# Strassen's seven products for eight in half of the gate and up matrix products of a transformer block

## The chip, the cores and the metric

The kernel runs on one core of a Trainium2 chip. The metric is the time of one execution on the device, in microseconds (us). The core has a matrix engine (TensorE, PE in the profile, whose weight loads are the row PEld), a vector engine (VectorE, DVE), a scalar engine (ScalarE, ACT), GpSimd (POOL) and a queue engine that issues DMAs (SyncE, SP). Each runs its own instructions in the order in which they were built.

## The reference

Two transformer blocks run one after the other on 512 tokens of width 1024, in float32. The change touches only the second block, which has two layers with two SwiGLU networks each, so four in all:

```python
def swiglu(x, w_gate, w_up, w_down):
    return (jax.nn.silu(x @ w_gate) * (x @ w_up)) @ w_down
...
    for l in range(DEPTH_2):
        h = h + 0.5 * swiglu(rmsnorm_2(h, ffn1_norm[l]), ffn1_w_gate[l], ffn1_w_up[l], ffn1_w_down[l])
        ...
        h = h + 0.5 * swiglu(rmsnorm_2(h, ffn2_norm[l]), ffn2_w_gate[l], ffn2_w_up[l], ffn2_w_down[l])
```

Gate and up are matrices of 1024 x 2816, down is 2816 x 1024.

## The kernel before

Activations lie as eight tiles of 128 x 512 (128 of the 1024 features by all 512 tokens). Every matrix product is made from three matmuls (`acc`, L384): each operand is split into a high and a low part (`split`: ScalarE copies the high part, L327, and VectorE subtracts it, L328), and high x low, low x high and high x high are summed in PSUM.

`swiglu_hidden` goes over the hidden features in 11 pairs of 128-row tiles (index `mp`, 0 to 10). For a pair, `proj_a` makes the gate product: two weight units, each of four k tiles by 256 columns, are loaded by a DMA into a tile `raw` (three buffers), split into `wh` and `wl` (three buffers each), and used by 2 x 4 x 3 matmuls of 512 columns; so a product has 48 matmuls. Then the up product follows in the same way. When a gate tile is done, VectorE multiplies it by the norm (`g`, L1203) and ScalarE applies silu; when an up tile is done, VectorE makes two multiplications (`u`, L1209 and L1210) and the product is split into `uh` and `ul`. After the eleventh pair, `residual` multiplies all 22 hidden tiles with down, 256 output columns at a time, and VectorE adds the result to `h`.

The order on each engine is made by a scheduler from the order of the code and the free buffers. VectorE therefore works on splits for weights that TensorE needs one or two units later, in the gaps between the multiplications that wait for TensorE.

## Time and profile before

| | |
|---|---|
| median of three runs | 3082.12 us (3081.68 to 3083.63) |
| the profiled execution | 3079.62 us, of which the span from first to last instruction is 3077.8 us |
| TensorE busy | 3011.2 us, 98% of the span |
| VectorE busy | 1734.0 us, 56% |
| ScalarE busy | 1159.8 us, 38% |

The profiled execution is 2.50 us shorter than the median of the three runs, and 1.8 us of it lie outside the span. Busy time of TensorE counts overlapping matmuls once. A matmul's duration is longer than the distance to the next one, since matmuls are pipelined; what a matmul costs is read from the distance of two starts.

### The profile page before, as it was taken

The page shows a single profiled execution, that of the slowest core. Times are in us where ns is not written, and L with a number is a line of the kernel's source. Part 1 is how long each engine was busy: PE and PEld are TensorE (multiplying, and loading weights), DVE is VectorE, ACT ScalarE, POOL GpSimd, SP SyncE. Part 2 cuts the span into 40 slices and gives each one's busy share as a digit, 9 for nine tenths or more (in the row PEclk, how much of TensorE's full clock was granted, in tenths as well). Part 3 has the DMA queues.
Part 4 walks back from the last instruction along what each step waited for, and adds up shares of the span by engine and source line. Part 5 has one row for each costly group of instructions (what it writes and reads, how often), then busy time and mean ns, then how long its engine had stood idle before and what let it go on. Part 6 is the DMA issues. An engine that isn't in the chain of part 4 may idle for free.

```text
span 3077.8 us, 37929 instructions
## 1 busy us (share of the span) xinstructions
PE 3011.2 (98%) x14805; PEld 2501.5 (81%) x14805; DVE 1734.0 (56%) x2770; ACT 1159.8 (38%) x1794; POOL 171.1 (6%) x150
## 2 busy tenths in 40 slices
PE   9999999999999999999999999999999999999998
PEld 7778777888888888778888888888888788888888
DVE  5678666666454443587654433644435885644437
ACT  4454534444333322335333322433323353333225
POOL 0000221111000000112000000000000120000000
PEclk9999999999999999999999999999999999999999
DMA  6354324333233333333333333333333224333224
GB/s 206 119 130 131 100 82 129 93 102 96 93 93 110 96 95 97 97 91 86 109 100 96 96 96 99 100 103 96 93 96 106 84 69 126 93 98 98 91 95 152
DMA packets 309061, 318.69 MB, mean 104 GB/s; under 512 B 25230, under 2 KB 284005, under 8 KB 308882
## 3 DMA queue, kind: packets, MB, share of 16 engines
q1 hardware_dynamic: 303502, 307.24, 33.7%
q10 hardware_dynamic: 5380, 9.03, 1.0%
q8 instruction: 116, 1.90, 0.3%
q14 instruction: 63, 0.52, 0.1%
HBM read 289.77 MB, written 7.96 MB: 97 GB/s over the span
## 4 chain that ended last, share of the span: by engine, by line
PE 86%; DVE 7%; issue 3%; DMA 2%; ACT 2%; SPq 1%; POOL 1%; DVEq 0%; ACTq 0%; POOLq 0%
PE w L384 78%; DVE wl L328 2%; PE p L1419 1%; ACT wh L327 1%; PE p L762 1%; PE p L1512 1%; PE p L1580 1%; PE p L723 0%; PE p L769 0%; PE p L509 0%; DMA raw<-in_w_in_dram 0%; PE p L725 0%; PE p L1400 0%; DMA vec<-t5rows 0%; PE p L770 0%
## 5 line engine op out<-in xcount | busy, mean ns | idle before, releaser
L328 DVE TENSOR_TENSOR wl<-raw,wh 128x1024 fp32r<-128x1024 f32 (+3 forms) x524 | 634.6, 1211 | 874.2 <-ACT wh L327 863.1
L384 PE MATMUL w<-xl,wh 128*128 128x512 f32 (+1 forms) x2584 | 1000.9, 387 | 0.0
L384 PE MATMUL w<-xh,wh 128*128 128x512 f32 (+1 forms) x2584 | 998.5, 386 | 0.0
L384 PE MATMUL w<-xh,wl 128*128 128x512 f32 (+1 forms) x2584 | 998.1, 386 | 0.0
L327 ACT ACTIVATE wh<-raw 128x1024 fp32r<-128x1024 f32 (+3 forms) x524 | 537.8, 1026 | 1120.8 <-PE w L384 846.7
L384 PEld LDWEIGHTS w<-xl,wh 128*128 128x128 f32 x2584 | 487.0, 188 | 92.1 <-issue 0.6
L384 PEld LDWEIGHTS w<-xh,wh 128*128 128x128 f32 x2584 | 486.4, 188 | 92.1 <-issue 0.2
L384 PEld LDWEIGHTS w<-xh,wl 128*128 128x128 f32 x2584 | 486.7, 188 | 90.2
L384 PE MATMUL w<-uh,wl 128*128 128x512 f32 x880 | 342.3, 389 | 0.0
L384 PE MATMUL w<-ul,wh 128*128 128x512 f32 x880 | 342.3, 389 | 0.0
L384 PE MATMUL w<-uh,wh 128*128 128x512 f32 x880 | 342.3, 389 | 0.0
L384 PEld LDWEIGHTS w<-uh,wh 128*128 128x128 f32 x880 | 165.2, 188 | 34.4
L384 PEld LDWEIGHTS w<-ul,wh 128*128 128x128 f32 x880 | 165.2, 188 | 34.3
L384 PEld LDWEIGHTS w<-uh,wl 128*128 128x128 f32 x880 | 165.2, 188 | 34.2
L384 PE MATMUL w<-wh,xl 128*128 128x256 f32 (+2 forms) x480 | 141.2, 296 | 2.8 <-ACT wh L327 2.4
L384 PE MATMUL w<-wl,xh 128*128 128x256 f32 (+2 forms) x480 | 139.6, 291 | 0.0
L384 PE MATMUL w<-wh,xh 128*128 128x256 f32 (+2 forms) x480 | 137.8, 291 | 0.0
L1203 DVE TENSOR_TENSOR g<-w,R 128x512 f32<-128x512 f32 x88 | 60.5, 691 | 112.5 <-PE w L384 94.2
L327 ACT ACTIVATE uh<-u 128x512 fp32r<-128x512 f32 x88 | 55.7, 634 | 151.1 <-DVE u L1210 151.1
L303 ACT ACTIVATE g<-g 128x512 f32<-128x512 f32 (+1 forms) x112 | 65.8, 593 | 110.1 <-DVE g L1203 96.7
L384 PEld LDWEIGHTS w<-wh,xl 128*128 128x128 f32 x480 | 92.5, 193 | 7.3 <-ACT wh L327 2.6
L384 PEld LDWEIGHTS w<-wl,xh 128*128 128x128 f32 x480 | 92.8, 193 | 1.5 <-issue 0.7
(394 smaller groups left out, 3222.7 us busy)
## 6 DMA issues: line engine op xcount, KB each, us to landing
raw<-in_ffn_w_gate_dram SPq DMA_DIRECT2D x88, 512.0 KB, 3.8
raw<-in_ffn_w_up_dram SPq DMA_DIRECT2D x88, 512.0 KB, 3.8
raw<-in_ffn_w_down_dram SPq DMA_DIRECT2D x80, 512.0 KB, 3.5
raw<-in_w_in_dram SPq DMA_DIRECT2D x71, 512.0 KB, 3.9
raw<-in_w_up_dram SPq DMA_DIRECT2D x44, 512.0 KB, 3.5
raw<-in_w_gate_dram SPq DMA_DIRECT2D x32, 512.0 KB, 3.5
raw<-in_ple_w_gate_dram SPq DMA_DIRECT2D x24, 512.0 KB, 3.6
raw<-in_w_down_dram SPq DMA_DIRECT2D x20, 512.0 KB, 3.5
```

The source lines that it names most:

```text
L303: self.members.append(self.nc.scalar.activation(*args, **kw).ins)
L327: nc.scalar.activation(hi, src, AF.Copy)
L328: nc.vector.tensor_tensor(lo, src, hi.bitcast(F32), op=OP.subtract)
L384: mm(out, l, r, start=first and i == 0, stop=last and i == 2, skip_group_check=shared)
L762: nc.tensor.transpose(pt[:, i * P:(i + 1) * P], y[:, s * P:(s + 1) * P], self.ident)
L1203: nc.vector.tensor_tensor(t, p, x.R, op=OP.mult)
L1419: nc.tensor.matmul(p[:, t * 64:(t + 1) * 64].rearrange("p (n w) -> p n w", w=w), x[:, t * P:(t + 1) * P], v(x)[:, t * nb:(t + 1) * nb, 1], ...
L1512: nc.tensor.matmul(po[:, t * 64:(t + 1) * 64], sc[s][:, (t - s) * P:(t - s + 1) * P], V[s][:, hv], start=s == 0, stop=s == t)
L1580: nc.tensor.matmul(p[:, :n], q[h][:96, t * P:(t + 1) * P], k[h][:96, :n], start=True, stop=True)
```

## The change

In each of the four SwiGLUs the 11 pairs are cut into three parts (`THIRDS`: pairs 0 to 3, 4 to 7 and 8 to 10), and down is multiplied after each part, with the 8, 8 and 6 hidden tiles of that part; so `h` is added to three times.

Pairs 0, 1 and 2 stay as they were. From pair 3 on the gate product, and in pairs 4, 6, 8 and 10 the up product too, is made by `seven`: the product is seen as two by two blocks (two halves of k, two row tiles, two halves of the tokens), and seven block products of 4 x 3 matmuls with 256 columns take the place of eight. That is 84 matmuls of 256 columns for 48 of 512. For it the weights need four differences (`minus`) and seven splits of 128 x 512, and three additions in PSUM on VectorE and two copies of PSUM (`keep`) on ScalarE join the seven results. The activations need four sums and differences of their blocks, which `half_sums` makes once for each SwiGLU, after pair 1: 16 operations of 128 x 256 and 8 splits of 128 x 512, and first eight full-precision tiles, on ScalarE where the source is still there (`x.src`), and on VectorE in the first SwiGLU (L440), where it isn't.

`beside` interleaves the steps of the gate product with those of the up product of the same pair, so that other matmuls stand between a block product and the step that needs what VectorE or ScalarE makes of it.

```diff
--- before.py
+++ after.py
@@ -91,6 +91,11 @@
 KEEP = 2
 EARLY = 3
 LATE = 5.0, 8.0
+FF_SLOTS = dict(U=16, S=16, B=16, V4=4)
+THIRDS = (0, 1, 2, 3), (4, 5, 6, 7), (8, 9, 10)
+BESIDE = 0, 0, 1, 0, 1, 0, 0
+BOTH = 0, 0, 3, 0, 2, 0, 0
+PLAIN, UP = 3, (4, 6, 8, 10)
 MA, MB, YN = 13, 13, 8
 RAW, SPL = 3, 3
 AHEAD, EVAC, BEHIND = 1000, -1000, 1000
@@ -248,8 +253,9 @@
         return f"{s}{self.n}"
 
     PLACE = {"h": "H", "mix": "H", "xh": "X", "xl": "X", "mh": "X", "ml": "X", "uh": "U", "ul": "U",
+             "sxh": "S", "sxl": "S", "wb": "B", "wt4": "V4",
              "qk": "W", "V": "W", "rc": "W", "hq": "Q", "yh": "Y", "yl": "Y", "oh": "Y", "ol": "Y", "gate": "G"}
-    SHORT = ("R", "sq", "g", "u", "hd", "cv", "rows", "out", "lv", "rst", "rt")
+    SHORT = ("sv", "R", "sq", "g", "u", "hd", "cv", "rows", "out", "lv", "rst", "rt")
 
     def S(self, name="s", dt=F32):
 
@@ -418,6 +424,109 @@
                 yield nk * 3 * ncol * PASS
 
 
+    def half_sums(self, x, after):
+
+
+        nc, tt = self.nc, self.nc.vector.tensor_tensor
+        out = [([], []) for _ in range(4)]
+        for g in range(2):
+            f = {}
+            for k in (2 * g, 2 * g + 1, 2 * g + 4, 2 * g + 5):
+                f[k] = self.S("uh")
+                with self.after(after):
+                    if x.src:
+                        nc.scalar.activation(f[k], x.src[k], AF.Copy, scale=x.gain(k))
+                    else:
+                        tt(f[k], x.hi[k].bitcast(F32), x.lo[k].bitcast(F32), op=OP.add)
+            s = [self.S("uh") for _ in range(4)]
+            for i in range(2):
+                a, b = f[2 * g + i], f[2 * g + i + 4]
+                one, two, c = slice(0, 256), slice(256, 512), slice(256 * i, 256 * i + 256)
+                tt(s[0][:, c], a[:, two], b[:, two], op=OP.add)
+                tt(s[1][:, c], s[0][:, c], a[:, one], op=OP.subtract)
+                tt(s[2][:, c], a[:, one], a[:, two], op=OP.subtract)
+                tt(s[3][:, c], b[:, one], s[1][:, c], op=OP.subtract)
+            for t, (hi, lo) in zip(s, out):
+                h, l = self.S("sxh", F32R), self.S("sxl", F32R)
+                self.split(t, h, l)
+                for y, z in ((hi, h), (lo, l)):
+                    y += [z[:, :256], z[:, 256:]]
+        return out
+
+    def seven(self, W, c0, x, sums, evac):
+
+        nc, tt = self.nc, self.nc.vector.tensor_tensor
+        raw = []
+        for k0 in (0, 4):
+            t = self.rp.tile([P, 1024], F32, name=self.nm("raw"), tag="raw").rearrange("p (k c) -> p k c", k=4)
+            nc.sync.dma_start(t, W[k0 * P:(k0 + 4) * P, c0:c0 + 256].rearrange("(k p) c -> p k c", p=P))
+            raw += [t[:, :, :P], t[:, :, P:]]
+        b11, b12, b21, b22 = raw
+        both = [self.wp.tile([P, 1024], F32R, name=self.nm(n), tag=n) for n in ("wh", "wl")]
+        four = lambda t: t.rearrange("p (k c) -> p k c", k=4)
+
+        def minus(a, b):
+            t = four(self.S("wt4"))
+            tt(t, a, b, op=OP.subtract)
+            return t
+
+        def parts(src, at=None):
+            if at is None:
+                hi, lo = (four(self.S("wb", F32R)) for _ in range(2))
+            else:
+                hi, lo = (four(t[:, at * T:(at + 1) * T]) for t in both)
+            self.split(src, hi, lo)
+            return hi, lo
+        one, two = slice(0, 256), slice(256, 512)
+        cut = lambda k0, c: tuple([t[:, c] for t in y[k0:k0 + 4]] for y in (x.hi, x.lo))
+        bank, other = self.wps(), self.wps()
+        X, y, z, v = bank[:, one], bank[:, two], other[:, one], other[:, two]
+
+        def product(out, b, a, first=False):
+            for k in range(4):
+                self.acc(out, b[0][:, k], b[1][:, k], a[0][k], a[1][k], first and k == 0, k == 3, shared=True)
+            return 4 * 3 * 256 * PASS
+
+        def keep(p):
+            t = self.S("sv")
+            nc.scalar.activation(t[:, one], p, AF.Copy)
+            return t[:, one]
+        t1 = minus(b12, b11)
+        B11, T1 = parts(b11, 0), parts(t1)
+        t2 = minus(b22, t1)
+        T2, B21 = parts(t2), parts(b21, 1)
+        T3, B22 = parts(minus(b22, b12)), parts(b22)
+        T4 = parts(minus(b21, t2))
+        time = product(X, B11, cut(0, one), True)
+        p1 = keep(X)
+        yield time
+        time = product(z, T1, sums[0], True)
+        p5 = keep(z)
+        yield time
+        time = product(y, T2, sums[1])
+        tt(y, y, p1, op=OP.add)
+        tt(z, y, p5, op=OP.add)
+        yield time
+        yield product(X, B21, cut(4, one))
+        time = product(y, T3, sums[2])
+        tt(v, y, p5, op=OP.add)
+        yield time
+        time = product(z, B22, sums[3])
+        evac(1, other)
+        yield time
+        time = product(y, T4, cut(4, two))
+        evac(0, bank)
+        yield time
+
+    def beside(self, long, short, at):
+
+        for i, t in enumerate(long):
+            yield t
+            for _ in range(at[i]):
+                yield next(short)
+        yield from short
+
+
     def columns(self, parts, dma):
 
         nc = self.nc
@@ -456,9 +565,11 @@
             self.net, self.gain, self.scales = net, gain, scales
             self.hi, self.lo = [None] * KD, [None] * KD
             self.acc = [None] * len(scales)
+            self.src = [None] * KD
 
         def add(self, k, t):
             net, nc = self.net, self.net.nc
+            self.src[k] = t
             if self.gain is not None:
                 self.hi[k], self.lo[k] = net.S("xh", F32R), net.S("xl", F32R)
                 net.split(t, self.hi[k], self.lo[k], self.gain(k))
@@ -1183,40 +1294,57 @@
             norm.R, R1 = self.broadcast(norm.both)
             for k, t in enumerate(h):
                 nc.vector.scalar_tensor_tensor(t, t, self.col("norm_final_g", k), R1, op0=OP.mult, op1=OP.mult)
+        norm.src = None
         self.later((LATE[0], rows), (LATE[1], tile))
         return norm
 
 
     def swiglu(self, h, norm, which, l, nxt):
-        with self.phase({"W": 8}, U=44):
+        with self.phase({"W": 8}, **FF_SLOTS):
             self.swiglu_hidden(h, norm(), which, l, nxt)
 
     def swiglu_hidden(self, h, x, which, l, nxt):
         nc, a = self.nc, self.a
         Wg, Wu, Wd = (a[f"{which}_w_{n}_2"][l] for n in ("gate", "up", "down"))
-        uh, ul = [], []
-        for mp in range(11):
-            g = []
-
-            def evac_g(j, p, g=g):
-                t = self.S("g")
-                nc.vector.tensor_tensor(t, p, x.R, op=OP.mult)
-                self.act("silu", t, t, AF.Silu)
-                g.append(t)
-
-            def evac_u(j, p, g=g):
-                u = self.S("u")
+        uh, ul = [None] * KF, [None] * KF
+        first = []
+
+        def work(mp, sums):
+            g = [None] * 2
+
+            def evac_g(j, p):
+                g[j] = self.S("g")
+                first.append(nc.vector.tensor_tensor(g[j], p, x.R, op=OP.mult).ins)
+                self.act("silu", g[j], g[j], AF.Silu)
+
+            def evac_u(j, p):
+                u, m = self.S("u"), mp * 2 + j
                 nc.vector.tensor_tensor(u, p, x.R, op=OP.mult)
                 nc.vector.tensor_tensor(u, u, g[j], op=OP.mult)
-                hi, lo = self.S("uh", F32R), self.S("ul", F32R)
-                self.split(u, hi, lo)
-                uh.append(hi)
-                ul.append(lo)
-            self.push(self.proj_a(Wg, KD, [(mp * 256, 256)], x.hi, x.lo, evac_g))
-            self.push(self.proj_a(Wu, KD, [(mp * 256, 256)], x.hi, x.lo, evac_u))
+                uh[m], ul[m] = self.S("uh", F32R), self.S("ul", F32R)
+                self.split(u, uh[m], ul[m])
+            up = self.proj_a(Wu, KD, [(mp * 256, 256)], x.hi, x.lo, evac_u)
+            at = BESIDE
+            if sums and mp in UP:
+                up, at = self.seven(Wu, mp * 256, x, sums, evac_u), BOTH
+            if sums is None:
+                yield from self.proj_a(Wg, KD, [(mp * 256, 256)], x.hi, x.lo, evac_g)
+                yield from up
+            else:
+                yield from self.beside(self.seven(Wg, mp * 256, x, sums, evac_g), up, at)
+        sums = None
+        for third in THIRDS:
+            for mp in third:
+                self.push(work(mp, sums))
+                self.drain()
+                if mp == PLAIN - 2:
+                    made = self.half_sums(x, first[:1])
+                if mp == PLAIN - 1:
+                    sums = made
+            k = slice(third[0] * 2, third[-1] * 2 + 2)
+            self.push(self.residual(Wd[k.start * P:k.stop * P], k.stop - k.start, uh[k], ul[k], h, 0.5,
+                                    nxt=nxt if third is THIRDS[-1] else None))
             self.drain()
-        self.push(self.residual(Wd, KF, uh, ul, h, 0.5, nxt=nxt))
-        self.drain()
 
     def layer_consts(self):
         t = self.S("layer")
```

The order of all instructions outside the four SwiGLUs stays as it is, apart from line and buffer numbers. Two places inside show what moves.

The first is the third pair (`mp` 2) of the first SwiGLU. On VectorE before, the split `wl1691`, the second weight unit of this pair's up product, stands between the multiplications of the second pair (`u1671`) and the gate tiles of the third pair (`g1682`):

```order
L1209 TENSOR_TENSOR u1671_8015<-w1661_7947,R1632_7784 128x512
L1210 TENSOR_TENSOR u1671_8015<-u1671_8015,g1659_7943 128x512
L328 TENSOR_TENSOR wl1688_8095<-raw1686_8092,wh1687_8094 128x1024
L328 TENSOR_TENSOR ul1673_8019<-u1671_8015,uh1672_8018 128x512
L328 TENSOR_TENSOR wl1691_8125<-raw1689_8122,wh1690_8124 128x1024
L1203 TENSOR_TENSOR g1682_8072<-w1674_8022,R1632_7784 128x512
L1203 TENSOR_TENSOR g1683_8087<-w1675_8023,R1632_7784 128x512
```

After the change the same weight unit is called `wl1723`, and stands here (`sx` are the splits of the sums of activations, `wb` and `wl1733` split blocks of the fourth pair's gate weights, `wt4` is a difference of such blocks):

```order
L334 TENSOR_TENSOR sxl1699_8079<-uh1694_8066,sxh1698_8078 128x512
L1317 TENSOR_TENSOR g1714_8144<-w1706_8094,R1632_7784 128x512
L334 TENSOR_TENSOR sxl1701_8083<-uh1695_8067,sxh1700_8082 128x512
L1317 TENSOR_TENSOR g1715_8159<-w1707_8095,R1632_7784 128x512
L334 TENSOR_TENSOR sxl1703_8087<-uh1696_8068,sxh1702_8086 128x512
L334 TENSOR_TENSOR wl1723_8197<-raw1721_8194,wh1722_8196 128x1024
L334 TENSOR_TENSOR sxl1705_8091<-uh1697_8069,sxh1704_8090 128x512
L334 TENSOR_TENSOR wl1733_8243<-raw1730_8238,wh1732_8242 128x512
L334 TENSOR_TENSOR wb1738_8251<-wt41736_8246,wb1737_8250 128x512
```

The work of `half_sums` has come between: from the second pair's first `u` to this split VectorE now has 42 instructions (24 of 128 x 512, 16 of 128 x 256 and 2 of 128 x 1024), where it had 8.

On TensorE before, at the step from the first to the second weight unit of the third pair's up product:

```order
L384 MATMUL w1685_8091<-xh1550_7271,wl1688_8095 128x512
L384 MATMUL w1685_8091<-xh1550_7271,wh1687_8094 128x512
L384 MATMUL w1684_8090<-xl1575_7447,wh1690_8124 128x512
L384 MATMUL w1684_8090<-xh1574_7446,wl1691_8125 128x512
L384 MATMUL w1684_8090<-xh1574_7446,wh1690_8124 128x512
L384 MATMUL w1684_8090<-xl1579_7464,wh1690_8124 128x512
```

and after:

```order
L390 MATMUL w1717_8163<-xh1550_7271,wl1720_8167 128x512
L390 MATMUL w1717_8163<-xh1550_7271,wh1719_8166 128x512
L390 MATMUL w1716_8162<-xl1575_7447,wh1722_8196 128x512
L390 MATMUL w1717_8163<-xl1575_7447,wh1722_8196 128x512
L390 MATMUL w1734_8244<-xl1519_7065,wh1732_8242 128x256
L390 MATMUL w1735_8245<-sxl1683_8043,wb1737_8250 128x256
L390 MATMUL w1716_8162<-xh1574_7446,wl1723_8197 128x512
L390 MATMUL w1716_8162<-xh1574_7446,wh1722_8196 128x512
```

The matmuls with `wh1722` and, of the fourth pair's gate, with `wh1732` and `wb1737` are taken first, one of each, and then `w1716` needs `wl1723`.

The second place is the fourth pair of the second SwiGLU. On TensorE the third block product of the gate is followed by the first weight unit of the plain up product (`w2963`, `w2964`):

```order
L390 MATMUL w2945_14541<-sxh2911_14379,wb2952_14554 128x256
L390 MATMUL w2945_14541<-sxh2911_14379,wb2951_14553 128x256
L390 MATMUL w2963_14617<-xl2789_13824,wh2966_14621 128x512
L390 MATMUL w2964_14618<-xl2789_13824,wh2966_14621 128x512
L390 MATMUL w2963_14617<-xh2788_13823,wl2967_14622 128x512
L390 MATMUL w2963_14617<-xh2788_13823,wh2966_14621 128x512
```

and on VectorE its split `wl2967` stands behind the up tiles of the third pair:

```order
L334 TENSOR_TENSOR wb2955_14562<-wt42953_14559,wb2954_14561 128x512
L334 TENSOR_TENSOR ul2937_14513<-u2935_14509,uh2936_14512 128x512
L1323 TENSOR_TENSOR u2938_14528<-u2938_14528,g2926_14456 128x512
L334 TENSOR_TENSOR wb2957_14566<-raw2942_14537,wb2956_14565 128x512
L470 TENSOR_TENSOR wt42958_14569<-raw2942_14537,wt42950_14551 128x512
L334 TENSOR_TENSOR ul2940_14532<-u2938_14528,uh2939_14531 128x512
L334 TENSOR_TENSOR wl2967_14622<-raw2965_14619,wh2966_14621 128x1024
L334 TENSOR_TENSOR wb2960_14572<-wt42958_14569,wb2959_14571 128x512
L507 TENSOR_TENSOR w2945_14541<-w2945_14541,sv2961_14587 128x256
```

From the second pair's first `u` to `wl2967` VectorE has 51 instructions here (32 of 128 x 512, 16 of 128 x 256, 3 of 128 x 1024). The third and the fourth SwiGLU have the same order as the second at this place.

## Rows read from the trace of the kernel before

**Rows 1.** The page: busy time by engine, and the chain that ended last

```profile
PE 3011.2 (98%) x14805; PEld 2501.5 (81%) x14805; DVE 1734.0 (56%) x2770; ACT 1159.8 (38%) x1794; POOL 171.1 (6%) x150
...
PE 86%; DVE 7%; issue 3%; DMA 2%; ACT 2%; SPq 1%; POOL 1%; DVEq 0%; ACTq 0%; POOLq 0%
PE w L384 78%; DVE wl L328 2%; PE p L1419 1%; ACT wh L327 1%; PE p L762 1%; PE p L1512 1%; PE p L1580 1%; PE p L723 0%; PE p L769 0%; PE p L509 0%; DMA raw<-in_w_in_dram 0%; PE p L725 0%; PE p L1400 0%; DMA vec<-t5rows 0%; PE p L770 0%
```

**Rows 2.** Windows, second SwiGLU, gate and up, then down: stretch, length, busy, clock

```profile
1571.00:1799.00 228.00, 228.00 (x1008) 188.81 (x1007) 106.88 (x127) 70.32 (x85) 0.00 (x0) 1.00 0.33 98
1800.00:1921.00 121.00, 121.00 (x535) 100.19 (x535) 41.49 (x48) 32.54 (x40) 0.00 (x0) 1.00 0.29 91
```

**Rows 3.** Timeline of TensorE, second SwiGLU, first and 51st of 51 matmuls

```profile
1640.26 0.39 PE L384 MATMUL w<-xh,wh 128*128 128x512 f32 x1
...
1651.59 0.39 PE L384 MATMUL w<-xh,wl 128*128 128x512 f32 x1
```

**Rows 4.** Timeline of TensorE, last stage, first and 51st of 51 matmuls

```profile
3027.00 0.28 PE L384 MATMUL w<-xh,wh 128*128 128x256 f32 x1
...
3033.00 0.28 PE L384 MATMUL w<-xh,wl 128*128 128x256 f32 x1
```

**Rows 5.** Timeline of VectorE, first SwiGLU, the second pair's up tiles

```profile
936.09 0.69 DVE L1209 TENSOR_TENSOR u<-w,R 128x512 f32<-128x512 f32 x1 [0.35 <-PE w L384]
936.82 0.69 DVE L1210 TENSOR_TENSOR u<-u,g 128x512 f32<-128x512 f32 x1
938.21 0.69 DVE L328 TENSOR_TENSOR ul<-u,uh 128x512 fp32r<-128x512 f32 x1 [0.70 <-ACT uh L327]
938.82 0.68 DVE L1209 TENSOR_TENSOR u<-w,R 128x512 f32<-128x512 f32 x1
939.53 0.69 DVE L1210 TENSOR_TENSOR u<-u,g 128x512 f32<-128x512 f32 x1
940.14 1.22 DVE L328 TENSOR_TENSOR wl<-raw,wh 128x1024 fp32r<-128x1024 f32 x1
941.28 0.68 DVE L328 TENSOR_TENSOR ul<-u,uh 128x512 fp32r<-128x512 f32 x1
```

**Rows 6.** Groups by shape over the whole span: operation, count, busy us, mean ns

```profile
L327 ACT ACTIVATE uh<-u 128x512 fp32r<-128x512 f32 x88 | 55.7, 634 | 151.1 <-DVE u L1210 151.1
...
L1334 ACT ACTIVATE V<-w,y 128x256 f32<-128x256 f32 x32 | 14.9, 468 | 14.2 <-PE w L384 14.1
...
L1750 DVE TENSOR_TENSOR g<-w,R 128x256 f32<-128x256 f32 x16 | 6.3, 419 | 2.5 <-PE w L384 2.5
```

**Rows 7.** Timeline of TensorE around its wait at 480 us, first block

```profile
479.80 0.39 PE L384 MATMUL w<-mh,wh 128*128 128x512 f32 x1
484.00 0.79 PE L384 MATMUL w<-ml,wh 128*128 128x512 f32 x1 [3.81 <-DVE ml L1103]
484.59 0.63 PE L384 MATMUL w<-mh,wl 128*128 128x512 f32 x1
...
489.28 0.48 PE L384 MATMUL w<-ml,wh 128*128 128x512 f32 x1
489.60 0.40 PE L384 MATMUL w<-mh,wl 128*128 128x512 f32 x1
```

**Rows 8.** Windows of that wait: busy of PE, PEld, DVE, ACT, POOL, then PEclk

```profile
481.00:482.00 1.00, 0.00 (x0) 0.00 (x0) 1.00 (x3) 0.00 (x0) 0.00 (x0) 1.00 0.41 156
482.00:483.00 1.00, 0.00 (x0) 0.00 (x0) 1.00 (x2) 0.00 (x0) 0.87 (x1) 0.82 0.12 37
...
484.00:485.00 1.00, 1.00 (x2) 0.82 (x3) 1.00 (x1) 0.06 (x1) 1.00 (x1) 0.50 0.46 162
```

**Rows 9.** DMA issues by source: count, KB each, median us from issue to landing

```profile
raw<-in_ffn_w_gate_dram SPq DMA_DIRECT2D x88, 512.0 KB, 3.8
raw<-in_ffn_w_up_dram SPq DMA_DIRECT2D x88, 512.0 KB, 3.8
```

## Prediction

> **What bounds the kernel now.** I read the page first. TensorE is busy for 98% of the span, VectorE for 56%, and 86% of the chain that ended last lies on TensorE, 78% on the one line that issues the matmuls of the weight products [rows 1]. Then the stretch that is changed: over 228 us of gate and up and 121 us of down of the second SwiGLU TensorE is busy all the time at a granted clock of 1.00, while VectorE works 106.9 and 41.5 us and ScalarE 70.3 and 32.5 us [rows 2]. So a matmul that goes away here shortens the span by its distance to the next, as long as VectorE, ScalarE and the DMAs deliver in time; they have room on the whole, and the question is whether they have it at each place.
>
> **What a matmul costs.** Its bar (0.39 us) is not its cost. Fifty distances of matmuls with 512 columns take 11.33 us, 0.2266 us each [rows 3]. Fifty with 256 columns take 6.00 us, 0.1200 us each [rows 4]; this is the last stage, with weights stationary and half a tile of activations moving, as the change has it. Half the columns therefore cost 53%, not 50%. A plain product costs 48 x 0.2266 = 10.88 us, one by seven 84 x 0.1200 = 10.08 us: 0.80 us less, where counting multiplications promises an eighth, 1.36 us. In a SwiGLU 12 of 22 products change (8 gate, 4 up), in four SwiGLUs 48: **38.4 us** of TensorE time go away. Against this the Trainium skill (TensorE: Matmul & The Clock Gate, section "Back-to-back issue gap") gives the gap of an isolated warm matmul as columns over 2.4 GHz plus 2.5 ns; by it the products would cost 10.36 and 9.17 us, and the gain would be 57 us. The rows say otherwise: 0.2266 and 0.1200 us leave 13 ns beside the columns, and the sum goes by them.
>
> **What VectorE pays.** Neighbours that don't wait for each other start 0.61 us apart with 512 columns (938.21 to 938.82) and 1.14 us with 1024 (940.14 to 941.28), 0.08 us less than their bars; one that reads its neighbour's result starts 0.72 us after it [rows 5]. With 256 columns I take the bar of 0.42 us [rows 6] less the same 0.08, 0.34 us, between 0.31 (half of 0.61) and 0.42. A product by seven asks for 4 differences, 7 splits and 3 additions, 11 x 0.61 + 3 x 0.34 = 7.7 us, in the place of two weight splits of 1.14. A plain pair costs VectorE 4 x 1.14 + 2 x 0.61 for gate and 2 x (0.72 + 0.61 + 0.61) for up, 9.7 us of TensorE's 21.8. A pair with the gate by seven costs 15.1 us of 21.0, one with both 20.5 us of 20.2. A pair with both is thus just over what VectorE can do, but a gate-only pair or a down part (192 matmuls, 43.5 us, with 8 x 1.14 + 8 x 0.61 = 14 us of splits and additions) stands on either side. ScalarE has 14 splits at 0.63 us and 4 copies of PSUM at 0.47 [rows 6], with silu and hidden splits 13 us: no bound. The 16 further additions into `h` in a SwiGLU, and the weight blocks for the next pair, lie under the down matmuls.
>
> **Where TensorE will wait: the third and fourth pair.** Let T be the start of the second pair's up product. VectorE's first `u` there needs 36 matmuls and starts 0.19 us after them (the bar less the distance, 0.16, and a little; in [rows 5] it waits for just that): T + 8.35. What stands before it in VectorE's queue is done by then, so the queue can't start on `half_sums` earlier.
>
> In the first SwiGLU 42 instructions stand from there to the end of `wl1723`: 24 x 0.61 + 16 x 0.34 + 2 x 1.14 = 22.4 us, and 1.2 us for waits on ScalarE and a dependent neighbour, as in [rows 5] (0.70 and 0.12, and again in part). It is done at T + 31.9. TensorE has 122 matmuls of 512 columns and 2 of 256 before the one that needs it, 122 x 0.2266 + 2 x 0.12, and comes at T + 27.9: a wait of **4.0 us**. Behind `wl1723` wait the block splits of the fourth pair and the first weight unit of its up product, so the queue stays late and a second wait of some 1.5 us would follow. A wait of 3.8 us has its price in the first block: the clock was 1.00 in its second microsecond, 0.82 in the third and 0.50, the lower of its two levels (1.2 of 2.4 GHz), when the matmuls came back [rows 8], and 12 distances then took 5.28 us where 12 x 0.2266 = 2.72 was due [rows 7]: **2.6 us** lost. In that slow time VectorE catches up, so I count it in place of the second wait. First SwiGLU: 6.6 us.
>
> In the other three ScalarE makes the eight full-precision tiles, and 51 instructions stand up to `wl2967`: 32 x 0.61 + 16 x 0.34 + 3 x 1.14 = 28.4 us, and 1.9 us of waits (the same 1.2, and 0.7 until TensorE has the third pair's second up tile). Done at T + 38.6; TensorE comes at T + 144 x 0.2266 + 36 x 0.12 + 2 x 0.2266 = T + 37.4: **1.2 us**, three times, 3.6 us; so short a wait left the clock at 1.00 [rows 8].
>
> **The second and third parts.** Here I followed the order of VectorE, ScalarE and the raw tiles' DMAs row by row with the same prices. After a pair with both products the additions into PSUM that let the next pair's fourth block product start are done 0.1 us before TensorE asks, elsewhere 2 to 8 us before. VectorE loses some 4 us in each gate-only pair to the landing of a raw tile (3.8 us from issue, [rows 9]) which could be asked for only after its buffer's last split; that lies inside its lead. I charge 0.4 us for each of eight parts, 3.2 us, with bounds of 0 and 1.5 us. At the turn to down, the hidden tiles are due 7 us after the last up matmul and ready after some 4: nothing, and without that cover 4 us in each of 12 turns.
>
> **Sum.** 38.4 - 6.6 - 3.6 - 3.2 = 25.0 us. Against the profiled execution, 3077.8 + 1.8 = 3079.6, that is 3054.6; the median lies 2.5 us above that execution, so **3057 us**, 0.8% faster.
>
> **Rivals.**
> - *VectorE pays its whole bars* (0.69, 1.23 and 0.42 us, [rows 5, 6]) where operands are strided blocks or neighbours depend. Then the queues above take 25.7 + 1.2 and 32.5 + 1.9 us, the waits become 7.4 and 5.3 us, each with 2.6 us of clock and the first with 2 us more behind it: 12.0 + 3 x 7.9 = 35.7 us, and 1 us for each later part, 8: nothing of 38.4 is left, 3087 us, no change that can be told or slightly slower. Against it: 0.61 and 1.14 in [rows 5], on such splits. The Trainium skill (VectorE: DVE Perf Modes, section "The DRAIN you can't avoid") says that the next operation does not start until the pipe is empty, but that one which isn't held starts earlier; 938.21 to 938.82 shows the earlier start. 0.10.
> - *The raw buffers become the bound (slower).* Seven holds two of the three raw tiles until its last block is split, where a plain unit gave its one back after one split. If VectorE's lead is used up, each of the 32 products in the pairs with both shows its landing of 3.8 us [rows 9]. It decides at 25.0 / 32 = 0.8 us shown for each, beyond which the kernel is slower; with half the landing, 1.9 us, it is 61 - 25 = 36 us slower, 3118 us. For it: the three buffers, and only 0.1 us of lead after a pair with both. Against: the lead is 2 us and more at the other places, and DMA is busy a third of the time [rows 2]. 0.07.
> - *No wait anywhere.* VectorE finds its gaps, or ScalarE's tiles come sooner: 38.4 us, 3044 us. 0.12. The skill's gap, 57 us and thus 3025 us with no wait, has 0.01: [rows 3, 4] were read in this kernel.
> - *In between*: waits of 4 us and a slow clock in all four SwiGLUs, 25 to 33 us of 38.4, 3069 to 3077 us: 0.08.
>
> **How the numbers follow.** My forecast, with waits between 6 and 22 us (3050 to 3066 us), has 0.62. A measurement of this kernel tells some 0.2%, 6 us, from no change. Faster by more than that: 0.62 + 0.13 + 0.07 of the in-between = 0.82. Within: 0.01 of the in-between, 0.08 of the whole bars and 0.01 of the buffers, 0.10. Slower: 0.02 + 0.06 = 0.08. The range goes from no wait at all, 3043, to the worst in-between, 3077; it leaves out the skill's gap, the whole bars and the buffers, 0.18.
>
> **What the profile after would show.** TensorE's distances 0.120 us in the block products (right) or above 0.13 (wrong); the longest wait in the SwiGLUs, about 4 us, in the third pair of the first, released by VectorE's split L334, with PEclk at 0.50 behind it and nowhere else in a SwiGLU; waits of about 1 us in the fourth pair of the others; gate pairs 5 to 11 without a wait over 0.5 us. VectorE busy some 85 us longer for each SwiGLU (12 x 5.4 for the products, 10 for the sums, 10 for `h`). The prediction is wrong if the fourth pairs wait more than 4 us in every SwiGLU, if TensorE waits for a raw DMA, or if the block products' matmuls are spaced wider.

## The result, and the profile after

The changed kernel takes 3056.47 us (median of three runs, 3053.71 to 3058.94); its ratio to the kernel before is 0.9921, with a 95% interval of 0.9907 to 0.9934. That is 0.8% or 25 us faster. The prediction was 3057 us.

The page of the changed kernel's profile, its shortest execution (3053.71 us, of which the span is 3051.9); against [rows 1]:

```profile
PE 2976.9 (98%) x16533; PEld 2554.6 (84%) x16533; DVE 2073.3 (68%) x3514; ACT 1323.8 (43%) x2186; POOL 170.2 (6%) x150
...
PE 82%; DVE 9%; issue 4%; ACT 2%; DMA 2%; SPq 0%; POOL 0%; DVEq 0%; POOLq 0%; ACTq 0%
...
raw<-in_ffn_w_gate_dram SPq DMA_DIRECT2D x88, 512.0 KB, 4.3
raw<-in_ffn_w_up_dram SPq DMA_DIRECT2D x88, 512.0 KB, 3.9
```

TensorE is still busy for 98% of a span that is 25.9 us shorter. The raw tiles of gate and up land 4.3 and 3.9 us after their issue, in place of 3.8 [rows 9]. VectorE has 339 us more, 85 for each SwiGLU, as forecast. Its share of the chain that ended last has risen from 7 to 9%.

The second and third parts show the price of a block product. These are windows of the first SwiGLU of the changed kernel, pairs 4 to 7 and pairs 8 to 10 (columns as in [rows 2]):

```profile
1032.24:1114.60 82.36, 82.36 (x601) 78.47 (x600) 60.95 (x101) 37.84 (x63) 0.00 (x0) 1.00 0.32 98
1158.12:1219.45 61.33, 61.33 (x469) 59.38 (x468) 46.18 (x77) 29.54 (x49) 0.00 (x0) 1.00 0.30 93
```

Part two has 504 matmuls of 256 columns and 96 of 512: 504 x 0.1200 + 96 x 0.2266 = 82.2 us by [rows 3, 4], 82.36 measured, with TensorE busy from end to end and a clock of 1.00. Part three: 420 and 48, 61.3 worked out, 61.33 measured. By the gap of an isolated matmul that the Trainium skill gives (TensorE: Matmul & The Clock Gate, section "Back-to-back issue gap"), part two would by an estimate have taken 504 x 0.1092 + 96 x 0.2158 = 75.8 us; the trace does not agree with it here. The windows of parts two and three are as long in the other three SwiGLUs.

What TensorE waited for in the changed kernel, from the first SwiGLU to the fourth: the group of waits for weight splits (us in total, how many, the longest).

```profile
PE w L390 <- DVE wl L334: 8.1, 5, 3.6
```

The five waits of that group in the timeline of TensorE, each in the brackets of the matmul that waited:

```profile
955.74 0.28 PE L390 MATMUL w<-sxl,wb 128*128 128x256 f32 x1
959.61 0.50 PE L390 MATMUL w<-xh,wl 128*128 128x512 f32 x1 [3.58 <-DVE wl L334]
959.95 0.39 PE L390 MATMUL w<-xh,wh 128*128 128x512 f32 x1
...
963.82 0.40 PE L390 MATMUL w<-xh,wl 128*128 128x512 f32 x1
...
972.36 0.50 PE L390 MATMUL w<-xh,wl 128*128 128x512 f32 x1 [1.32 <-DVE wl L334]
...
1628.62 0.50 PE L390 MATMUL w<-xh,wl 128*128 128x512 f32 x1 [1.67 <-DVE wl L334]
...
2038.52 0.50 PE L390 MATMUL w<-xh,wl 128*128 128x512 f32 x1 [0.75 <-DVE wl L334]
...
2696.43 0.50 PE L390 MATMUL w<-xh,wl 128*128 128x512 f32 x1 [0.74 <-DVE wl L334]
```

The 3.58 us stand in the third pair of the first SwiGLU, before the matmul with `wl1723`, and 1.32 us more in its fourth pair; the others are in the fourth pairs of the other three. The timeline of VectorE before the first of them:

```profile
936.33 0.69 DVE L1322 TENSOR_TENSOR u<-w,R 128x512 f32<-128x512 f32 x1 [0.35 <-PE w L390]
...
946.16 0.42 DVE L447 TENSOR_TENSOR uh<-uh 128x256 f32<-128x256 f32 x1
946.49 0.42 DVE L448 TENSOR_TENSOR uh<-uh,uh 128x256 f32<-128x256 f32 x1
...
957.74 0.68 DVE L334 TENSOR_TENSOR sxl<-uh,sxh 128x512 fp32r<-128x512 f32 x1
958.34 1.22 DVE L334 TENSOR_TENSOR wl<-raw,wh 128x1024 fp32r<-128x1024 f32 x1
```

And the windows of a microsecond around its end, with the clock third from the right:

```profile
959.00:960.00 1.00, 0.39 (x2) 0.35 (x3) 1.00 (x2) 0.00 (x0) 0.00 (x0) 1.00 0.00 0
960.00:961.00 1.00, 1.00 (x5) 0.80 (x4) 1.00 (x3) 0.00 (x0) 0.00 (x0) 0.68 0.28 35
961.00:962.00 1.00, 1.00 (x4) 0.81 (x3) 1.00 (x3) 0.00 (x1) 0.00 (x0) 0.50 0.72 205
```

The prediction's T is the first row's start less 8.35, 927.98. VectorE ends `wl1723` at 959.56, T + 31.6 (forecast 31.9); TensorE asks at 956.02, T + 28.0 (forecast 27.9). The clock fell to 0.50 after TensorE had come back, and the eleven distances from 959.61 to 963.82 take 1.7 us more than 11 x 0.2266.

The idle time of the five waits and this 1.7 us make 9.8 us. What they cost is a little more: idle time is counted from the end of a bar, and bars are longer than distances. The starts of the matmuls give the whole loss. The table has the time from the first matmul of pair 0 to the end of pair 3 (to the next start behind its 384 or 420 matmuls), in the two timelines:

| SwiGLU | first | second | third | fourth |
|---|---|---|---|---|
| before, us | 89.99 | 88.12 | 88.74 | 88.12 |
| changed kernel, us | 96.37 | 89.44 | 89.05 | 88.39 |

One product by seven should have made each of these 0.8 us shorter; so 7.2, 2.1, 1.1 and 1.1 us are lost, 11.5 in all. Parts two and three lose 0.18 us in each SwiGLU, 0.7 in all, and 38.4 - 11.5 - 0.7 = 26.2 us are left.

Outside these products the two executions differ as well. The changed one takes 2.5 us less between them. Of this, 1.6 us lie before the second SwiGLU, where the clock fell for 3.4 us in the execution before (0.66 from 1294 to 1299 us) and did not in this one (1.00 from 1292 to 1297). It takes 0.2 us more ahead of the first SwiGLU and 2.6 us more in the last stage. There the first transposes wait 1.93 us for a small input, where they waited 0.94 us before, and the clock is lower behind it. The first of them in the timeline of TensorE:

```profile
2980.78 0.46 PE L683 MATMUL p<-ident,pin 128*128 128x128 f32 x2 [1.93 <-DMA pin<-in_p_dram]
```

### The profile page after: what moved, and what is told of

The parts are those of the page before. It is cut to its first block, busy times and chain, and to the rows that moved or that the text cites. A ratio compares the mean times of both kernels' runs of the same rounds, so it can differ in the third digit from the quotient of the medians.

```text
span 3051.9 us, 42727 instructions
## 1 busy us (share of the span) xinstructions
PE 2976.9 (98%) x16533; PEld 2554.6 (84%) x16533; DVE 2073.3 (68%) x3514; ACT 1323.8 (43%) x2186; POOL 170.2 (6%) x150
## 4 chain that ended last, share of the span: by engine, by line
PE 82%; DVE 9%; issue 4%; ACT 2%; DMA 2%; SPq 0%; POOL 0%; DVEq 0%; POOLq 0%; ACTq 0%
PE w L390 74%; DVE wl L334 2%; PE p L1547 1%; ACT wh L333 1%; PE p L873 1%; PE p L1640 1%; PE p L1708 1%; PE p L834 1%; PE p L880 0%; PE p L620 0%; PE p L836 0%; PE p L1528 0%; DMA dec<-in_decay_dram 0%; PE p L881 0%; PE p L1005 0%
## 5 line engine op out<-in xcount | busy, mean ns | idle before, releaser
L390 PE MATMUL w<-xh,wl 128*128 128x512 f32 (+1 forms) x2200 | 810.3, 368 | 8.1 <-DVE wl L334 8.1
L390 PE MATMUL w<-xl,wh 128*128 128x512 f32 (+1 forms) x2200 | 811.5, 369 | 0.0
L390 PE MATMUL w<-xh,wh 128*128 128x512 f32 (+1 forms) x2200 | 809.7, 368 | 0.0
L390 PEld LDWEIGHTS w<-xl,wh 128*128 128x128 f32 x2200 | 417.1, 190 | 62.3 <-issue 0.6
L390 PE MATMUL w<-sxh,wb 128*128 128x256 f32 x1536 | 282.0, 283 | 0.0
L390 PEld LDWEIGHTS w<-sxh,wb 128*128 128x128 f32 x1536 | 239.5, 192 | 0.6
L390 PE MATMUL w<-sxl,wb 128*128 128x256 f32 x768 | 217.4, 283 | 0.0
L333 ACT ACTIVATE wb<-wt 128x512 fp32r<-128x512 f32 x192 | 120.8, 630 | 121.4 <-DVE wt L470 87.2
L390 PEld LDWEIGHTS w<-sxl,wb 128*128 128x128 f32 x768 | 147.4, 192 | 0.7
L334 DVE TENSOR_TENSOR wb<-wt,wb 128x512 fp32r<-128x512 f32 x192 | 131.4, 684 | 13.2 <-ACT wb L333 13.2
```

The costliest lines, as they stand in the source:

```text
L333: nc.scalar.activation(hi, src, AF.Copy)
L334: nc.vector.tensor_tensor(lo, src, hi.bitcast(F32), op=OP.subtract)
L390: mm(out, l, r, start=first and i == 0, stop=last and i == 2, skip_group_check=shared)
```

## Experiments

Each run is given by its ratio to the kernel before, with a 95% interval, and its median. Kernels of one group ran on one chip, with the kernel before beside them: its median is 3080.4 to 3081.4 us in these groups and 3082.1 beside the changed kernel, so runs of different groups are compared by their ratios. The expectations are as they stood before the run. Cut places are marked in the edits by three points.

### Where the waits come from

**The sums in two halves** (`half_sums` gets the group `g` and the lists to append to):

```diff
+SUMS = ((0, (0,)), (1, (1,)))
...
-                if mp == PLAIN - 2:
-                    made = self.half_sums(x, first[:1])
+                for at, g in SUMS:
+                    if mp == at:
+                        self.half_sums(x, first[:1], g, made)
```

> half_sums is cut in two: the sums of its first four tiles are made after pair 0, those of the other four after pair 1; nothing else changes. Theory A (what the prediction says: TensorE waits because 42 or 51 instructions of VectorE, 15 us of them the sums in one lump, stand ahead of a weight split that TensorE needs next): half the lump is 7.5 us, less than VectorE's lead, so the 3.6, 1.3, 1.7, 0.75 and 0.75 us waits and the half clock (1.7 us) go; in the first SwiGLU, where VectorE is held until 919 us by the norm, about 1 us of wait comes in the second pair. Sum -8.8 us against the changed kernel: 3048 us, ratio to the kernel before 0.989. Rival B (VectorE is too loaded in the fourth pair, wherever the sums stand): the waits of the fourth pairs, 1.3, 1.7, 0.75 and 0.75 us, stay and only the 3.6 us and its clock go: 3051 us.

Measured: 0.9885 (0.9872 to 0.9899), 3044.3 us. None of the five waits is left in the trace; what waits stay in the SwiGLUs, 0.47 us in the first and 0.37 us in the third near their beginning, the kernel before has too (0.43 and 0.37). Pairs 0 to 3 take 89.45, 87.38, 87.98 and 87.38 us, 11.1 us less than in the changed kernel; by the ratios it is 0.0036 x 3082 = 11.1 us, with an interval of some 6 us either way. The wait expected in the second pair is missing by a hair, in the timeline of TensorE:

```profile
933.74 1.07 PE L391 MATMUL w<-xl,wh 128*128 128x512 f32 x4
934.67 0.50 PE L391 MATMUL w<-xh,wl 128*128 128x512 f32 x1
```

and in that of VectorE:

```profile
932.77 0.70 DVE L335 TENSOR_TENSOR sxl<-uh,sxh 128x512 fp32r<-128x512 f32 x1
933.37 1.24 DVE L335 TENSOR_TENSOR wl<-raw,wh 128x1024 fp32r<-128x1024 f32 x1
```

The split ends at 934.61; TensorE takes four matmuls that need only `wh` first, and starts the one with `wl` at 934.67. The fourth pairs have as much work for VectorE as before, and wait no more: rival B falls.

**The lump moved forward by one pair:**

```diff
-                if mp == PLAIN - 2:
+                if mp == PLAIN - 3:
```

> All of half_sums is made after pair 0, in one lump, one pair earlier than in the changed kernel; nothing else changes. Theory A (the lump in the queue): in the first SwiGLU the lump of 15 us now stands ahead of the second weight unit of the second pair's up product, VectorE starts on it later (its first u is held until 919 us by the norm), and the wait there is 8 to 9 us with 1.7 us of half clock, in place of 3.6 + 1.3 + 1.7; in the other three SwiGLUs ScalarE makes the full tiles, VectorE has a lead of some 4 us at that place, and their waits of 1.7, 0.75 and 0.75 us go. Sum: +3.5 - 3.2, so 3057 us, the same as the changed kernel. Rival B (VectorE's load in the third and fourth pair): all waits go, 3047 us.

Measured: 0.9931 (0.9917 to 0.9944), 3056.9 us, the same as the changed kernel. The one wait left for a split is in the second pair of the first SwiGLU, in TensorE's timeline:

```profile
944.34 0.79 PE L390 MATMUL w<-xh,wl 128*128 128x512 f32 x1 [7.36 <-DVE wl L334]
```

It is 7.4 us where 8 to 9 were expected, and the nine distances behind it (to 948.35, at a clock of 0.50) cost another 2.0 us. The other waits are gone. With the run before it, this shows that the waits come from the lump's place in VectorE's queue, not from how much VectorE has to do.

**Parts only, and sums made but not used.** For the first `PLAIN` is 99, so that no pair is made by seven and no sums are made; for the second:

```diff
-                if mp == PLAIN - 1:
+                if mp == 99:
                     sums = made
```

> No product is made by seven and no sums are made; what is left of the change is down in three parts, with 16 more additions into h in each SwiGLU. Theory A (the additions and the turns lie under down's matmuls): 3082 us, the same as before. Rival (hidden tiles come late at each turn to down, 4 us in 8 more turns): 3114 us.

> As the run before, but half_sums is made after pair 1 and its results are not used; all products are plain. Theory A (the sums cost what stands behind them in VectorE's queue): the wait of 3.5 us in the third pair of the first SwiGLU with 1.7 us of half clock, as in the changed kernel; the second wait (1.3 us) and those of the fourth pairs (0.75 us) are gone or shorter, since the fourth pair asks less of VectorE: 5 us over the run before, 3087 us. Rival (the sums cost their whole VectorE time, 15 us in the first SwiGLU and 10 in the others): 45 us over it, 3127 us.

Measured: parts only 0.9999 (0.9991 to 1.0008), 3082.0 us; with the sums 1.0014 (1.0005 to 1.0023), 3085.9 us. Down in three parts with its 64 more additions costs nothing that can be told. The window of part two of the first SwiGLU, with four plain pairs:

```profile
1026.53:1113.57 87.04, 87.04 (x385) 72.10 (x384) 39.26 (x46) 26.04 (x31) 0.00 (x0) 1.00 0.31 97
```

The sums cost 4.6 us by the ratios, with an interval of some 4 us either way, and not the 45 us of VectorE time. The trace shows where: pairs 0 to 3 take 94.68 us for 90.09 in the first SwiGLU and at most 0.3 us more in the others. It is one wait, 2.75 us where 3.5 were expected, in the third pair, and the clock behind it; TensorE's timeline of that run:

```profile
958.00 0.50 PE L390 MATMUL w<-xh,wl 128*128 128x512 f32 x1 [2.75 <-DVE wl L334]
```

### What a product is worth, and whether the raw buffers bound

**Gate only:**

```diff
-PLAIN, UP = 3, (4, 6, 8, 10)
+PLAIN, UP = 3, ()
```

> No up product is made by seven; the gate products of pairs 3 to 10 still are. 16 products go back to 48 matmuls of 512 columns: +16 x 0.80 = 12.8 us. The waits at the third pair stay as they are; the wait in the fourth pairs too, since the fourth pair has no up by seven in either kernel. Theory A (0.80 us for each product, no other cost in pairs 4 to 10): 3056.5 + 12.8 = 3069 us. Rival B (the pairs with both lose something that the trace doesn't show as idle time, say half a microsecond each): 3069 - 8 = 3061 us. By counted multiplications (1.36 us for each) it would be 3078 us.

Measured: 0.9958 (0.9946 to 0.9971), 3067.7 us: 11.3 us over the changed kernel by the medians, 0.0037 x 3082 = 11.4 by the ratios, 0.7 us for each of 16 products, against 0.80 from the distances. The interval of this difference is some 6 us either way, which leaves out counted multiplications (21.8 us) and, only just, rival B (4.8 us). The trace tells them apart better; part two of its first SwiGLU:

```profile
1031.89:1115.97 84.08, 84.08 (x529) 76.32 (x528) 52.94 (x82) 32.99 (x52) 0.00 (x0) 1.00 0.30 95
```

This is 1.72 us more than the changed kernel's 82.36, for two products that are plain again: 0.86 each. Rival B asks for 0.6 us and counted multiplications for 2.7. The five waits stay, as expected (3.45, 1.32 and three of 0.75 us).

**Up by seven in every pair from 4:**

```diff
-PLAIN, UP = 3, (4, 6, 8, 10)
+PLAIN, UP = 3, (4, 5, 6, 7, 8, 9, 10)
```

> The up product too is made by seven in every pair from 4 to 10 (pairs 5, 7 and 9 are added): 12 more products, 12 x 0.80 = 9.6 us less on TensorE. A pair with both asks 20.4 us of VectorE and 20.2 of TensorE. Theory A (raw buffers show once VectorE's lead is used up): in part two the third and fourth pair, in part three the third, show about 3.4 us each (what VectorE waited for raw tiles in one pair with both: 2.2 + 0.9 + 0.3), 4 x 3 x 3.4 = 41 us: 3088 us. Rival B (only VectorE's work counts): 0.25 us for each pair and some 1.5 us for each SwiGLU, 3053 us. Waits in A are released by VectorE's splits, with VectorE in turn waiting for a raw DMA.

Measured: 0.9898 (0.9884 to 0.9911), 3048.0 us. My theory A fell by 40 us. Rival B's 3053 us is not left out: the ratio gives 3050.7 us for a kernel before of 3082.1, 4 us either way. What B adds in the later pairs is not there, though. The window of part two of the first SwiGLU, now four pairs with both products:

```profile
1037.08:1117.71 80.63, 80.63 (x673) 80.63 (x672) 72.69 (x126) 43.23 (x77) 0.00 (x0) 1.00 0.34 109
```

672 x 0.1200 = 80.64: no stall at all, with VectorE busy 72.7 us of it. The waits in the third and fourth pairs stay as in the changed kernel (3.45, 1.33 and three of 0.75 us). The groups of VectorE that wait for raw tiles (count, busy, mean, idle before) say what was wrong. The changed kernel's:

```profile
L470 DVE TENSOR_TENSOR wt<-raw,wt 128x512 f32<-128x512 f32 x96 | 66.1, 688 | 58.7 <-DMA raw<-in_ffn_w_gate_dram 32.5 <-DMA raw<-in_ffn_w_up_dram 25.9
```

and this run's:

```profile
L470 DVE TENSOR_TENSOR wt<-raw,wt 128x512 f32<-128x512 f32 x120 | 82.8, 690 | 40.6 <-DMA raw<-in_ffn_w_gate_dram 25.5 <-DMA raw<-in_ffn_w_up_dram 14.1
```

With more products VectorE waits less for raw tiles. But ScalarE, which makes the high parts, waits more; its waits for raw tiles of gate and up (us in total, how many, the longest) in the changed kernel:

```profile
ACT wh L333 <- DMA raw<-in_ffn_w_up_dram: 6.6, 10, 1.5
ACT wh L333 <- DMA raw<-in_ffn_w_gate_dram: 3.3, 8, 0.7
```

and in this run:

```profile
ACT wh L333 <- DMA raw<-in_ffn_w_up_dram: 25.4, 14, 3.2
ACT wh L333 <- DMA raw<-in_ffn_w_gate_dram: 9.7, 14, 1.4
```

By the groups shown the two engines together waited 69 us for raw tiles in the changed kernel and 76 here, and in the window above none of it reached TensorE. In these places they were ahead of TensorE, and the idle time was room, not cost. I had added it to VectorE's work as if it went on.

**Two raw buffers in place of three** (on top of the run with both edits, below):

```diff
-RAW, SPL = 3, 3
+RAW, SPL = 2, 3
```

> The run with both edits (half_sums in two, up by seven in every pair from 4), with two raw buffers in place of three in the whole kernel. This prices the rival of the raw buffers. Theory A (VectorE shows the landing of a raw tile once no buffer is left ahead): a product by seven holds both buffers until its last block is split, the next raw tile is asked for only then and lands 3.5 to 4.3 us later; a pair with both costs VectorE 20.4 + 2 x 3.9 = 28 us for TensorE's 20.2, and after the lead of about one product the two last pairs of part two and the last of part three show 8 us each and more, 4 x 3 x 8 = 96 us or more: above 3130 us, and TensorE waits in parts two and three for splits that wait for raw. Rival B (the third buffer is not what hides the landing): no change, 3035 us. Plain stages ask for a unit every 5.4 us, more than landing and split together, and lose nothing by either.

Measured: 0.9917 (0.9901 to 0.9932), 3054.6 us: 20 us slower than with three, where theory A said 96 and more. TensorE's longest group of waits in the SwiGLUs is now for copies of PSUM in the middle of a product; from its groups of waits:

```profile
PE w L391 <- ACT sv L492: 3.0, 6, 0.9
```

Behind the two longest of them, of 0.9 us, stands a raw DMA after all, in ScalarE's queue. ScalarE's timeline just before the second of the two:

```profile
1746.80 0.63 ACT L334 ACTIVATE wh<-raw 128x512 fp32r<-128x512 f32 x1 [2.08 <-DMA raw<-in_ffn_w_up_dram]
1747.34 0.61 ACT L334 ACTIVATE uh<-u 128x512 fp32r<-128x512 f32 x1
1747.86 0.64 ACT L492 ACTIVATE sv<-w 128x256 f32<-128x256 f32 x2
```

and TensorE's:

```profile
1748.27 0.39 PE L391 MATMUL w<-sxl,wb 128*128 128x256 f32 x1 [0.92 <-ACT sv L492]
```

The eight windows of parts two and three take 8.0 us longer than with three buffers (the second part of the second SwiGLU 84.06 us for 80.63). By the profiled executions 8.6 of the 20 us lie in the last stage, after the fourth SwiGLU. The small rest is spread over the other stages, where single executions differ by as much. So both theories are off: the landing of a raw tile does come through once a buffer is gone, by way of ScalarE more than VectorE (their waits for raw tiles of gate and up rise from 32 to 105 us and from 40 to 60), but with 8.0 us for 56 products it is far less than a landing for each.

### How far it can be taken

**Both edits**, the sums in halves and up by seven in all pairs from 4:

> Two edits together: half_sums cut in two (after pair 0 and after pair 1) and the up product by seven in every pair from 4 to 10. Theory A (a block product costs its matmuls and nothing else; waits come from the lump of sums alone): both gains add, 9.8 us from the waits and 9.6 us from 12 more products, 3056.5 - 19.4 = 3037 us, ratio to the kernel before 0.985, and no wait in any SwiGLU. Rival (VectorE at 20.4 us for 20.2 of TensorE in seven pairs falls behind when no wait in the third pair has given it time to catch up): waits of some us in parts two and three, 3043 us or more.

Measured: 0.9851 (0.9838 to 0.9865), 3034.8 us, with none of the five waits left. The gains add. No run is faster than this one, 22 us under the changed kernel.

**Up by seven in pair 3 too** (`UP = (3, 4, ..., 10)`):

> As the run before, and the up product of pair 3 by seven too: 4 more products, 3.2 us less on TensorE. From the second pair's first u VectorE has 24.3 us until the third pair ends, and by the order of its queue some 25.5 us of work before the fourth pair's up blocks. Theory A (VectorE's queue decides by its place): 1 to 3 us of wait in the fourth pair of each SwiGLU, so nothing is gained or a little is lost against the run before: 3037 to 3042 us. Rival (the lead covers it, as it covered the pairs with both): 3034 us and no wait.

Measured: 0.9852 (0.9837 to 0.9867), 3035.4 us, and no new wait in a SwiGLU either. My wait of 1 to 3 us did not come. Pairs 0 to 3 take 88.75, 86.51, 87.14 and 86.51 us, where the run without the edit has 89.45, 87.38, 87.98 and 87.38: 0.70 to 0.87 us less, the price of one product each, 3.3 us in all. In the whole time this can't be told, with an interval of 4.6 us either way, and the profiled execution lost as much elsewhere: behind a wait of 0.95 us in a later stage the clock went down for 7 us, which the run without the edit does not show at that place. The wait in TensorE's timeline:

```profile
2523.00 0.33 PE L834 MATMUL p<-rk,rk 128*128 128x128 f32 x1 [0.95 <-DVE rs L1634]
```

and the windows on either side of the clock's fall:

```profile
2515.00:2524.00 9.00, 7.71 (x57) 6.87 (x56) 2.93 (x6) 3.23 (x5) 1.27 (x1) 1.00 0.49 140
2524.00:2532.00 8.00, 8.00 (x42) 7.71 (x41) 2.64 (x5) 0.84 (x3) 0.00 (x0) 0.57 0.42 110
```

So the step shortens the SwiGLUs as it should; whether it helps the whole kernel stays open.

**Only two plain pairs** (`PLAIN, UP = 2, (2, 3, ..., 10)`):

> As the run with both edits (half_sums in two, up by seven in every pair), but the products by seven begin with pair 2, gate and up, so only pairs 0 and 1 are plain: against the run before last (up by seven from pair 3) 2 x 4 = 8 more products, 6.4 us less on TensorE. The second half of the sums follows the second pair's up tiles, which VectorE begins 8.35 us after that product's start; its sums, splits and those multiplications take some 11.5 us, so they are done at about 20 us, where TensorE's second block product of pair 2 asks for them at 10.9 + 1.4 = 12.3 us. Theory A (place in the queue): a wait of some 8 us with 1.7 us of half clock in each of four SwiGLUs, 39 us lost for 6.4: 3067 us. Rival (other matmuls of the pair fill the time): 3029 us.

Measured: 0.9930 (0.9918 to 0.9943), 3057.5 us, 22 us slower than with three. Groups of TensorE's waits in the four SwiGLUs:

```profile
PE w L391 <- DVE sxl L335: 11.0, 4, 6.6
PE w L391 <- DVE wl L335: 6.1, 5, 1.8
```

The direction was right, the size not: in the first SwiGLU the sums are 6.6 us late where 8 were expected, in the others, where ScalarE makes the full tiles, 1.0 to 1.7 us, behind 1.8 us for a weight split. These waits are only part of the loss. In each SwiGLU the clock falls to 0.50 behind them, for 10 us in the first and 7 us in the others, which cost some 12 us by an estimate, half of the 23.8 us that TensorE worked at that clock. The window in the first SwiGLU:

```profile
952.00:964.00 12.00, 7.43 (x36) 7.14 (x37) 11.64 (x23) 6.22 (x13) 0.00 (x0) 0.57 0.17 50
```

The profiled execution is the slowest of five (3065.3 us). The third plain pair is the cover under which the sums are made.

## Why the prediction was right, point by point

- **What a product costs** (0.80 us less for each of 48): right. Part two takes 82.36 us for 82.2 worked out, the run with all up products 80.63 for 80.64, and parts only shows 87.04 us for the same four pairs with plain products. Half the columns are not half the time, and the counted eighth was never there.
- **What VectorE pays** (0.61, 0.34, 1.14 us apart): right. The step that I had only bounded, 256 columns, is 0.33 us (946.16 to 946.49), and `wl1723` ended 0.3 us ahead of the forecast after 42 instructions. The rival of whole bars falls with it.
- **First SwiGLU, 6.6 us**: 6.6 measured as idle time and clock, 7.2 by the starts, but by other terms. The wait was 3.6 us for 4.0 and the clock cost 1.7 for 2.6; the second wait, which I had let the slow clock swallow, came all the same, 1.3 us for 1.5. The step "VectorE catches up in the slow time" failed: 1.7 us of it were not enough. That the total is so near is luck.
- **The other three, 1.2 us each**: 1.7, 0.75 and 0.75 us idle, 3.2 in all for 3.6, and 4.3 by the starts. The 1.7 us have a cause that I left out of this stretch: in the second SwiGLU VectorE waited for the raw tile of the fourth pair's gate, and `wl2967` ended at 1628.57, T + 39.3 for 38.6 (T is 1589.26 there). VectorE's timeline there:

```profile
1602.44 0.69 DVE L470 TENSOR_TENSOR wt<-raw 128x512 f32<-128x512 f32 x1 [1.43 <-DMA raw<-in_ffn_w_gate_dram]
```

In the third and fourth this wait is 0.16 us or none. In gate only and in up by seven in every pair, which have the same order at that place, it is absent, and all three waits of TensorE are 0.75 us.

- **Parts two and three, 3.2 us**: 0.13 and 0.05 us in each SwiGLU, 0.7 in all. This was the worst-sized term. I took VectorE's idle time for raw tiles as something that might come through; it was the sign of a lead.
- **The raw buffers as the bound**: falls. Its break-even of 0.8 us per product was not come near to in the kernel as changed, where a late raw tile reached TensorE once, with some 0.9 us, nor with 12 products more; even with two buffers it costs 8.0 us in these products and 20 us in the whole kernel.
- **Signs of being wrong**: none came. The longest wait in a fourth pair is 1.67 us, TensorE itself waited for no raw DMA in a SwiGLU, the block products' matmuls stand 0.120 us apart, and the clock fell in no other place of a SwiGLU.
- **Not foreseen**: 2.6 us in the last stage of the profiled execution, and 2.5 us the other way between the products. The wait for `pin` is 0.9 to 1.9 us long in the profiles of these kernels, which have the same instructions there. I take it for a spread between executions; as each kernel has one profile, this is not shown.

The forecast took 13.4 us of waits from 38.4; 12.2 were measured, 0.6 and 0.7 us more in the two terms of waits and 2.5 us less in the parts. So the mechanism held, and 26.2 us stand against 25.0. That the whole execution comes as near, 25.9 us, is in part luck, as the differences outside these products nearly cancel. The rival with no wait at all had 3044 us; the sums in two halves then measured 3044.3.

## What to carry to other kernels

Price a cheaper matrix algorithm by the measured distance of its smaller matmuls, not by counted multiplications: here half the columns cost 53%, and of an eighth only 7% of a product was left. Work that an otherwise idle engine makes in one lump costs what stands behind the lump in its queue; cut it to below the lead of that queue, and 15 us of it were free. Idle time of an engine that waits for a buffer while it is ahead is room and not a cost; don't add it to its work. The room ends with the lead: with one buffer less, a raw tile's landing reached TensorE through the copies that stood behind it in ScalarE's queue.

## What the runs showed of the hardware

The clock fell after TensorE had come back, not during the wait: 1.00 in the last microsecond of the 3.6 us wait, 0.50 from about 960.4 us on. In [rows 8], and in the 7.4 us wait of the lump moved forward, it fell within the wait (0.76 from 941 to 942 us, 0.50 from 942 to 943). Behind waits of 1.3 and 1.7 us in the changed kernel's SwiGLUs the distances stayed at 0.23 us, while behind one of 0.95 us in a stage with many small gaps it fell to its lower level for 7 us. So the length of the last wait alone did not decide it in these traces.
